# First block sums issued by GpSimd behind output tiles, and attention's token statistics behind a quarter of the second pair's products

## The chip, the core and the metric

The kernel runs on one NeuronCore of a Trainium2 chip. A core has five engines, each with its own in-order stream of instructions: TensorE (PE in the profile, with its weight loads as PEld) multiplies matrices into PSUM, VectorE (DVE) and ScalarE (ACT) do arithmetic on tiles, GpSimd (POOL) does some arithmetic, and SyncE (SP) does nothing but issue DMAs. GpSimd issues DMAs as well; those that add to their destination (accumulate) are issued there. The metric is device microseconds of one launch. A measurement of this kernel spreads over some 0.4%.

## The reference

A decoder trunk of two layers on 512 tokens with 16 learned meta tokens put in front (528 in all), width 1024, everything in float32. Each layer is a mixer and a gated MLP, each behind an RMS norm and added to the residual h:

```python
h = concatenate([meta, x])                      # 528 x 1024
# layer 0: forgetting attention, 16 heads of 64
q, k, v, f, o = split(rms_norm(h) @ w_in)
q, k = rms_norm(q), rms_norm(k)                 # per head
c = cumsum(log_sigmoid(f + b_f))
s = q.k / 8 + c_t - c_s  (causal);  a = softmax(s) v
h = h + (a * sigmoid(o)) @ w_out
# layer 1: HGRN2, 8 heads of 128, chunks of 64
S_t = diag(f_t) S_{t-1} + k_t v_t^T;  o_t = S_t^T q_t;  gated, projected, added to h
# after each mixer: ConvFFN, hidden width 2816
a = causal_conv3(rms_norm(h) @ w_gate)
h = h + (silu(a) * (rms_norm(h) @ w_up)) @ w_down
```

The output is the last 512 tokens of h.

## The kernel before

All of h stays in SBUF as eight tiles of 128 features by 528 tokens. A product of float32 accuracy is made of three fp32r matmuls: weight and input are each split into a high part (a cast on ACT) and a low part (a subtraction on DVE, `sub`, line 126), and hi·hi, hi·lo and lo·hi are summed in PSUM (`proj_unit`, lines 250, 253 and 254). A weight is so loaded (SP), cast (ACT) and subtracted (DVE) before its matmuls run. The raw buffers that the loads write are few, and the next load of a kind waits until the subtraction has read the one before. The tokens' RMS factor is not applied to the input but to the product: `sumsq` adds squares over the eight tiles into `ss`, `token_stats` (lines 350 and 352) sums over the partitions with narrow matmuls, a chain of small DVE operations makes the reciprocal root, and `spread_rs` (line 371) spreads it over partitions into `rsb`.

**Attention** (`fox`) runs over eight pairs of heads. `stage_a(p)` makes q and k of a pair (two weights, two token halves: four PSUM tiles of 24 matmuls each), `stage_v` the values, `stage_f` the forget gates, `stage_l` and `stage_t` the softmax. `weave` deals these generators out against each other: each yields the cost of a step, and the one that has done the smallest share of its stated cost goes next. The tile scheduler then sets the order on each engine by its own rules. Before the first pair, the statistics of the tokens are made: `token_stats`, two more matmuls for the row form (line 430), four DMAs into `et`, and `spread_rs`; all of this stands in the program ahead of pair 0 and waits for the last square of h. The first pair's products have four PSUM tiles of their own, and pair 1's q takes the banks "p" when those come free. At the end, `out_proj(m)` multiplies the gated heads by wo for the eight output tiles in the order m = 4, 0, 1, 2, 3, 5, 6, 7: the tiles 0 to 3 are mostly done already and need a weight of 128 KB each; 4 to 7 take one of 512 KB.

**The MLP** (`ffn`) computes most of its pairs of hidden tiles by Strassen's scheme: seven products of half-size blocks in place of eight (`seven`, lines 1183 to 1185). Four of the seven left operands are sums of two weight blocks. `make_sums` forms them by DMA alone, with no engine's arithmetic: a plain load of one block of 256 KB (line 225, on SP) into a room, then a second block, or an earlier sum, accumulated onto it (line 226, on POOL). A job (one pair's gate or up half) has four sums: 1 and 3 from the weights, 2 as an accumulate of sum 1, 4 as an accumulate of sum 2. There are eleven rooms, used in turn. `make_sums` is a generator that is stepped by `next(self.making)`; a step forms one or two sums. Six steps are taken before the MLP starts: in attention at the start of six of the output tiles, in the HGRN mixer at the start of the output tiles 2 to 7. The further steps are taken inside `seven`, when a job's sums have been cast (line 1160). The first pair of hidden tiles is computed plainly (`plain`, line 1255 is the end of its up half), and Strassen's pairs follow. `new_pair` clears two columns of a tile A on GpSimd (line 1236), in the first MLP only.

## Time and profile before

| | |
|---|---|
| three runs | 1447.70, 1450.93, 1453.36 us |
| the profiled execution | 1452.92 us |
| its span | 1451.1 us, mean granted clock 0.994 |
| PE busy | 1420.7 us (98%) |
| DVE, ACT, POOL busy | 1010.1, 724.3, 164.3 us |
| moved by DMA | 206.9 MB, mean 143 GB/s |

Attention takes the first 392 us of the span, the first MLP up to about 760, HGRN up to about 1096, the second MLP the rest. "Idle before, releaser" in a row is how long the engine stood still ahead of an instruction and what ended that. A DMA's time "to landing" runs from its issue to the last byte. The granted PE clock is given as a share of full speed.

### The profile page before, as it was taken

The numbers are of one execution on the slowest core, as the hardware profiler recorded it, in microseconds if no ns is written. First come the engines' busy times: TensorE is split into PE (matmuls) and PEld (weight loads), VectorE is DVE, ScalarE is ACT, GpSimd is POOL, SyncE is SP. The second block draws the span as 40 slices with busy tenths as digits, with TensorE's granted clock in tenths as the row PEclk, the third lists the DMA queues.
The fourth block names the chain that finished last, engine by engine and source line by source line (L and its number), as shares of the span: only waits on it lengthen the run. The fifth ranks groups of instructions, "written<-read, shape, count | busy, mean of one in ns | idle before, by whom it ended". The sixth has DMA issues, their size and how long they took to land.

```text
span 1451.1 us, 29767 instructions
## 1 busy us (share of the span) xinstructions
PE 1420.7 (98%) x11368; PEld 1339.2 (92%) x11368; DVE 1010.1 (70%) x2282; ACT 724.3 (50%) x1528; POOL 164.3 (11%) x273
## 2 busy tenths in 40 slices
PE   7999999999899999999999999999999999999998
PEld 6898888899899999999999999999999899999997
DVE  6545455775698886767775667677656987777774
ACT  5356554663566554554543224333435665555551
POOL 4000000001012222221000000000100222221100
PEclk9999999999999999999999999999999999999999
DMA  4424344335659898886322202222643899989833
GB/s 161 120 63 134 76 124 123 89 99 150 182 138 232 231 238 203 205 214 165 97 61 87 88 2 88 61 72 74 170 122 84 206 256 220 237 214 222 203 90 101
DMA packets 105463, 206.90 MB, mean 143 GB/s; under 512 B 14168, under 2 KB 18008, under 8 KB 105320
## 3 DMA queue, kind: packets, MB, share of 16 engines
q1 hardware_dynamic: 82280, 163.05, 36.9%
q0 software_dynamic: 23040, 41.95, 17.5%
q8 instruction: 89, 1.46, 0.4%
q14 instruction: 54, 0.44, 0.1%
HBM read 168.53 MB, written 2.10 MB: 118 GB/s over the span
## 4 chain that ended last, share of the span: by engine, by line
PE 91%; DMA 4%; DVE 2%; ACT 2%; SPq 1%; issue 1%; DVEq 0%; ACTq 0%
PE pss L250 7%; PE pss L254 7%; PE pss L253 7%; PE psp L250 7%; PE psp L253 7%; PE psp L254 7%; PE psp L301 6%; PE psp L1183 5%; PE psp L1184 5%; PE psp L1185 5%; PE psd L1183 3%; PE psd L1184 3%; PE psd L1185 3%; PE psc L816 2%; PE pss L974 1%; PE psc L1183 1%
## 5 line engine op out<-in xcount | busy, mean ns | idle before, releaser
L126 DVE TENSOR_TENSOR lo<-raw,hi 128x512 fp32r<-128x512 f32 (+2 forms) x322 | 252.8, 790 | 79.8 <-ACT hi L1160 39.9
L250 PE MATMUL psp<-xhi,hi 128*128 128x264 f32 (+2 forms) x784 | 228.1, 292 | 6.2 <-ACT xhi L326 6.2
L253 PE MATMUL psp<-xlo,hi 128*128 128x264 f32 (+2 forms) x784 | 226.4, 289 | 0.0
L254 PE MATMUL psp<-xhi,lo 128*128 128x264 f32 (+2 forms) x784 | 225.9, 289 | 0.0
L1160 ACT CAST hi<-raw 128x512 fp32r<-128x512 f32 (+1 forms) x232 | 139.2, 604 | 170.4 <-PE pss L253 58.6
L253 PE MATMUL pss<-room,hi 128*128 128x264 f32 (+2 forms) x532 | 169.7, 320 | 0.0
L254 PE MATMUL pss<-room,lo 128*128 128x264 f32 (+2 forms) x532 | 168.8, 320 | 0.0
L250 PE MATMUL pss<-room,hi 128*128 128x264 f32 (+2 forms) x532 | 168.1, 320 | 0.0
L250 PEld LDWEIGHTS psp<-xhi,hi 128*128 128x128 f32 x784 | 149.9, 192 | 9.8 <-ACT xhi L326 6.2
L200 ACT CAST hi<-raw 128x1024 fp32r<-128x1024 f32 (+2 forms) x86 | 83.1, 968 | 145.0 <-PE psp L253 63.9
L253 PEld LDWEIGHTS psp<-xlo,hi 128*128 128x128 f32 x784 | 149.7, 191 | 2.2 <-issue 2.1
L254 PEld LDWEIGHTS psp<-xhi,lo 128*128 128x128 f32 x784 | 149.2, 191 | 2.0 <-issue 1.9
L1183 PE MATMUL psp<-xhi,hi 128*128 128x264 f32 (+1 forms) x480 | 136.4, 284 | 3.4 <-ACT hi L1160 2.7
L1185 PE MATMUL psp<-xhi,lo 128*128 128x264 f32 (+1 forms) x480 | 136.2, 284 | 0.9 <-DVE lo L126 0.9
L1184 PE MATMUL psp<-xlo,hi 128*128 128x264 f32 (+1 forms) x480 | 135.7, 283 | 0.0
L1160 ACT CAST hi<-two 128x512 fp32r<-128x512 f32 x118 | 72.9, 619 | 84.5 <-PE psd L1184 33.0
L254 PEld LDWEIGHTS pss<-room,lo 128*128 128x128 f32 x532 | 100.1, 189 | 6.3
L253 PEld LDWEIGHTS pss<-room,hi 128*128 128x128 f32 x532 | 100.2, 188 | 5.2
L250 PEld LDWEIGHTS pss<-room,hi 128*128 128x128 f32 x532 | 99.5, 188 | 4.2
L1307 DVE TENSOR_TENSOR h<-h,pss 128x264 f32<-128x264 f32 (+2 forms) x145 | 73.6, 508 | 36.3 <-PE pss L254 35.9
L1183 PEld LDWEIGHTS psp<-xhi,hi 128*128 128x128 f32 x480 | 90.7, 189 | 6.5 <-ACT hi L1160 4.0
L1183 PE MATMUL psd<-xfhi,hi 128*128 128x264 f32 (+1 forms) x320 | 90.8, 284 | 1.3 <-ACT hi L1160 0.7
(485 smaller groups left out, 3939.3 us busy)
## 6 DMA issues: line engine op xcount, KB each, us to landing
raw<-gu SPq DMA_DIRECT2D x136, 256.0 KB
two<-gu SPq DMA_DIRECT2D x118, 256.0 KB
raw<-dn SPq DMA_DIRECT2D x80, 256.0 KB
two<-gu POOLq DMA_DIRECT2D x58, 256.0 KB, 6.8
one<-gu SPq DMA_DIRECT2D x42, 256.0 KB
two<-two POOLq DMA_DIRECT2D x40, 256.0 KB, 5.0
pk<-stg SPq DMA_DIRECT2D x30, 264.0 KB
raw<-wqk SPq DMA_DIRECT2D x14, 512.0 KB
```

Source lines behind the costliest of these rows:

```text
L126: self.nc.vector.tensor_tensor(out, x, y, ALU.subtract)
L200: nc.scalar.copy(hi, raw)
L250: ins = mm(ps, hi[:, i, :], xh, start=k == 0, stop=False)
L253: mm(ps, hi[:, i, :], xl, start=False, stop=False)
L254: mm(ps, lo[:, i, :], xh, start=False, stop=k == total - 1)
L301: mm(ps[:tn, :256], y[:, t0 : t0 + tn], w, start=n == 0, stop=n == 23)
L816: ins = mm(o, v[:, j, 2 * (p % 2) + hd, :], w[hd][0], start=j == 0, stop=j == last)
L1160: nc.scalar.copy(hi, raw)
L1183: mm(ps, hi[:, k, :], xh, start=start and k == 0, stop=False, skip_group_check=not start)
L1184: mm(ps, hi[:, k, :], xl, start=False, stop=False, skip_group_check=not start)
L1185: mm(ps, lo[:, k, :], xh, start=False, stop=k == 3, skip_group_check=not start)
L1307: nc.vector.tensor_tensor(hv, hv, ps, ALU.add)
```

## The change

Two things are altered.

*Token statistics.* They become a function `stats` that `stage_a(0)` calls after it has copied its own row of squares, so that they stand behind pair 0's products in the program. Their matmuls get an order (without a semaphore) behind `self.product`, the last matmul that `proj_unit` has written so far. The work of the first two turns of the loop is dealt out by hand: `stage_a(0)` up to a cost of 10.6, then `stage_a(1)` up to 2.6, which is the first of its four PSUM tiles, then the rest of `stage_a(0)`; `stage_a(1)` goes on in the next turn. Pair 1's products take banks "s", as the statistics do, in place of "p".

*Block sums.* While `self.pace` is set, `new` first copies one column of the tile `pace` into the room on GpSimd, and issues the plain load on GpSimd too. The load overwrites the column, so that it has to wait for the copy, and the copy waits for the tile. `pace` is the last column of the output tile of h that has just been done. The steps are taken at the ends of output tiles: five in attention (after tiles 3, 4, 5, 6 and 7, in the order in which they run), five in HGRN (after 0, 2, 4, 6 and 7), and the sixth in `plain` behind its first up half, with `pace` a column of t. Then `pace` is cleared, and the further loads are issued on SP as before. Six steps form nine sums.

```diff
         def new(job, f, x, y):
             s = made[job, f] = next(rooms)
-            nc.sync.dma_start(s, x)
+            if self.pace is None:
+                nc.sync.dma_start(s, x)
+            else:
+
+                nc.gpsimd.tensor_copy(s[:, 0:1], self.pace)
+                nc.gpsimd.dma_start(s, x)
             nc.gpsimd.dma_start(s, y, accum_op=ALU.add)
...
-                mm(ps, lo[:, i, :], xh, start=False, stop=k == total - 1)
+                self.product = mm(ps, lo[:, i, :], xh, start=False, stop=k == total - 1)
...
-            nc.tensor.matmul(ps[:, t, :], self.ss[:, t0 - i0 : t0 - i0 + P], self.onesd, start=True, stop=True)
+            ins = nc.tensor.matmul(ps[:, t, :], self.ss[:, t0 - i0 : t0 - i0 + P], self.onesd, start=True, stop=True)
+            if prev is not None:
+                self.after(ins, prev)
...
-        am, rs = self.token_stats(SEG0, True, start)
         et = sp.tile([64, 33], F32, name="et")
-        ssr = s2.tile([2, T], F32, name="ssr", tag="strow", bufs=1)
-        for t0, tn in full:
-            sr = start()
-            mm(sr[:2, :tn], self.onesd, self.ss[:, t0 : t0 + tn], start=True, stop=True)
-            nc.vector.tensor_copy(ssr[:, t0 : t0 + tn], sr[:2, :tn])
...
+        def stats():
+
+            nonlocal rs
+            _, rs = self.token_stats(SEG0, True, start, self.product)
...
+            self.spread_rs(rs, SEG0, start)
...
-                    ps = banks[i] if banks else bank()
+                    ps = banks[i] if banks else start() if p == 1 else bank()
...
             yield 0.9
+            if p == 0:
+                stats()
...
-            if p + 3 < NPAIR:
+            if p == -3:
+
+                first, second = stage_a(0), stage_a(1)
+                fill += [take(first, 10.6), take(second, 2.6), first]
+                cost += 15.5
+            elif p == -2:
+                fill.append(second)
+                cost += 10.2
+            elif p + 3 < NPAIR:
...
-            for step, _ in enumerate(out_proj(m, 6 if m < NEARLY else 0, KT, res)):
-                if i > 1 and step == 0:
-                    next(self.making)
+            for _ in out_proj(m, 6 if m < NEARLY else 0, KT, res):
+                pass
             self.sumsq(m, first=NEARLY)
+            self.pace = self.h[:, m, T - 1 :]
+            if m >= NEARLY - 1:
+                next(self.making)
...
         for m in range(KT):
-            if m > 1:
-                next(self.making)
...
             self.sumsq(m, A1)
+            self.pace = self.h[:, m, T - 1 :]
+            if m in (0, 2, 4, 6, 7):
+                next(self.making)
...
                 input_forms(2 * m + 1)
+                self.pace = t[:, 0, n - 1 : n]
+                if m == 0:
+                    next(self.making)
+            self.pace = None
             split(t, out)
```

How the instructions stand now, at three places. First TensorE at the start, where pair 0's products end (psd); before, the statistics (pss from ss) follow at once:

```order
L250 MATMUL psd<-xhi,hi 128x264
L253 MATMUL psd<-xlo,hi 128x264
L254 MATMUL psd<-xhi,lo 128x264
L350 MATMUL pss<-onesd,ss 128x2 x5
L352 MATMUL pss<-onesd,ss 16x2
L430 MATMUL pss<-ss,onesd 2x264 x2
L544 MATMUL psd<-sqq,hsel 32x264
L250 MATMUL psp<-xhi,hi 128x264
```

and in the changed kernel, behind 24 rows of products into pss of which these are the last three, and ahead of the values (line 306):

```order
L255 MATMUL pss<-xhi,hi 128x264
L258 MATMUL pss<-xlo,hi 128x264
L259 MATMUL pss<-xhi,lo 128x264
L355 MATMUL pss<-onesd,ss 128x2 x5
L359 MATMUL pss<-onesd,ss 16x2
L443 MATMUL pss<-ss,onesd 2x264 x2
L559 MATMUL psd<-sqq,hsel 32x264
L306 MATMUL psp<-hi,xhi 128x256
```

The statistics moved back by 24 products. Lines 350, 352, 430 and 544 of before are 355, 359, 443 and 559 of the change. From the first MLP on, TensorE's order is the same in both.

Second SP's queue at the end of attention (wo is the output weight, gu the gate and up weights; `one` and `two` hold the rooms), before:

```order
L199 DMA raw<-wo 128x256
L225 DMA one<-gu 128x512
L199 DMA raw<-wo 128x256 x2
L199 DMA raw<-wo 128x1024
L225 DMA two<-gu 128x512 x2
L199 DMA raw<-wo 128x256
L225 DMA two<-gu 128x512 x6
L199 DMA raw<-wo 128x256 x3
L724 DMA res<-h 128x528
L199 DMA raw<-wo 128x1024 x3
```

and now:

```order
L226 DMA one<-gu 128x512 x2
L199 DMA raw<-wo 128x256 x2
L199 DMA raw<-wo 128x1024
L199 DMA raw<-wo 128x256 x4
L749 DMA res<-h 128x528
L199 DMA raw<-wo 128x1024 x3
```

Eleven loads of sums stood among the wo weights; two are left, ahead of them, and nine have gone to GpSimd. In HGRN the same nine have left the places between that mixer's output weights.

Third GpSimd's queue from there on, before, where each row is the accumulate of a sum, with the clears of A:

```order
L226 DMA one<-gu 128x512
L226 DMA two<-gu 128x512 x4
L226 DMA two<-two 128x512
L226 DMA two<-gu 128x512
L226 DMA two<-two 128x512 x2
L226 DMA one<-two 128x512 x2
L1236 MEMSET A 128x2x2 x2
```

and now the last step of the nine, the one that waits for t:

```order
L229 COPY two<-t 128x1
L229 COPY one<-t 128x1
L230 DMA two<-gu 128x512
L230 DMA one<-gu 128x512
L231 DMA two<-two 128x512
L231 DMA two<-gu 128x512
L231 DMA one<-gu 128x512
L231 DMA two<-two 128x512
L231 DMA one<-two 128x512
L231 DMA two<-gu 128x512
L231 DMA two<-one 128x512
L1264 MEMSET A 128x2x2
```

Line 229 is the paced copy, 230 the plain load, 231 the accumulate. All later accumulates and clears stand behind these copies in the same queue.

More of the change, by code (lines that the diff above doesn't have):

```diff
@@ L343, in rsqrt, with token_stats @@
         return y
-    def token_stats(self, segs, last=False, bank=None):
+    def token_stats(self, segs, last=False, bank=None, prev=None):
         nc = self.nc
@@ L349, in token_stats @@
         for t, (t0, _, i0, _) in enumerate(segs):
-            nc.tensor.matmul(ps[:, t, :], self.ss[:, t0 - i0 : t0 - i0 + P], self.onesd, start=True, stop=True)
+            ins = nc.tensor.matmul(ps[:, t, :], self.ss[:, t0 - i0 : t0 - i0 + P], self.onesd, start=True, stop=True)
+            if prev is not None:
+                self.after(ins, prev)
         if last:
-            nc.tensor.matmul(ps[:16, 5, :], self.ss[:, 512:528], self.onesd, start=True, stop=True)
+            ins = nc.tensor.matmul(ps[:16, 5, :], self.ss[:, 512:528], self.onesd, start=True, stop=True)
+            self.after(ins, prev)
         am = self.cp.tile([P, 6], F32, name="am", tag="am", bufs=2)
@@ L424, in fox @@
         start = partial(self.bank, "s")
-        am, rs = self.token_stats(SEG0, True, start)
         et = sp.tile([64, 33], F32, name="et")
-        ssr = s2.tile([2, T], F32, name="ssr", tag="strow", bufs=1)
-        for t0, tn in full:
-            sr = start()
-            mm(sr[:2, :tn], self.onesd, self.ss[:, t0 : t0 + tn], start=True, stop=True)
-            nc.vector.tensor_copy(ssr[:, t0 : t0 + tn], sr[:2, :tn])
-        for g in range(4):
-            t0, tn = full[g % 2]
-            nc.sync.dma_start(et[16 * g : 16 * g + 16, :], ssr[:, t0 : t0 + tn].rearrange("r (j c) -> r j c", c=33))
-        nc.vector.tensor_scalar(et, et, EPS, EPS, ALU.add, ALU.mult)
-        self.spread_rs(rs, SEG0, start)
+        rs = None
+        def stats():
+            nonlocal rs
+            _, rs = self.token_stats(SEG0, True, start, self.product)
+            ssr = s2.tile([2, T], F32, name="ssr", tag="strow", bufs=1)
+            for t0, tn in full:
+                sr = start()
+                ins = mm(sr[:2, :tn], self.onesd, self.ss[:, t0 : t0 + tn], start=True, stop=True)
+                self.after(ins, self.product)
+                nc.vector.tensor_copy(ssr[:, t0 : t0 + tn], sr[:2, :tn])
+            for g in range(4):
+                t0, tn = full[g % 2]
+                nc.sync.dma_start(et[16 * g : 16 * g + 16, :], ssr[:, t0 : t0 + tn].rearrange("r (j c) -> r j c", c=33))
+            nc.vector.tensor_scalar(et, et, EPS, EPS, ALU.add, ALU.mult)
+            self.spread_rs(rs, SEG0, start)
         rcol = [0, 1, 2, 3, 5]
```

## The prediction

> **What bounds the kernel now.** I read the page's busy times and chain first, then the PE timeline for every idle stretch, then the windows and the DMA rows round each of them.
>
> ```profile
> PE 1420.7 (98%) x11368; PEld 1339.2 (92%) x11368; DVE 1010.1 (70%) x2282; ACT 724.3 (50%) x1528; POOL 164.3 (11%) x273
> PE 91%; DMA 4%; DVE 2%; ACT 2%; SPq 1%; issue 1%; DVEq 0%; ACTq 0%
> ```
>
> TensorE is the bound. The span is 1451.1 us and PE is busy for 1420.7 of it, so all idle time together is 30 us, the first 6.2 of it before anything has landed. A change that adds no matmul, as this one, can only take or give PE idle time, and time at the reduced clock. The matmuls named here stand where that idle time is (its length and its releaser in brackets):
>
> ```profile
> 20.64 0.28 PE L254 MATMUL psd<-xhi,lo 128*128 128x264 f32 x1
> 23.61 1.28 PE L350 MATMUL pss<-onesd,ss 128*128 128x2 f32 x10 [2.69 <-DVE ss L318]
> 68.11 0.38 PE L483 MATMUL psc<-tot,cst 128*128 128x2 f32 x2 [1.40 <-DVE tot L481]
> 187.10 0.44 PE L779 MATMUL pss<-identr,lr 128*128 128x128 f32 x1 [1.96 <-DVE rqq L342]
> 270.24 0.36 PE L573 MATMUL psd<-rows,selr 128*128 128x264 f32 x1 [1.57 <-DMA rows<-yr]
> 363.76 0.39 PE L250 MATMUL pss<-pk,hi 128*128 128x264 f32 x1 [1.38 <-ACT hi L200]
> 368.68 0.39 PE L250 MATMUL psp<-pk,hi 128*128 128x264 f32 x1 [1.41 <-ACT hi L200]
> 372.57 0.39 PE L250 MATMUL pss<-pk,hi 128*128 128x264 f32 x1 [2.15 <-ACT hi L200]
> ```
>
> Some of these idle stretches cost twice. In the windows below the columns are busy time and count of PE, PEld, DVE, ACT and POOL, then the granted PE clock, the DMA share and the GB/s.
>
> ```profile
> 22.50:25.80 3.30, 2.19 (x17) 1.64 (x18) 3.20 (x10) 2.96 (x8) 0.00 (x0) 1.00 0.48 161
> 25.80:29.20 3.40, 3.40 (x16) 1.91 (x14) 3.03 (x20) 0.15 (x1) 0.00 (x0) 0.50 0.01 1
> 29.20:32.60 3.40, 3.40 (x32) 3.15 (x27) 1.00 (x4) 0.38 (x1) 0.00 (x0) 1.00 0.01 2
> 66.70:70.10 3.40, 2.00 (x17) 1.99 (x17) 3.09 (x15) 1.42 (x3) 0.00 (x0) 1.00 0.67 225
> 370.60:374.00 3.40, 0.82 (x5) 0.61 (x5) 3.40 (x7) 2.53 (x4) 0.48 (x1) 0.99 1.09 274
> 374.00:377.40 3.40, 3.40 (x16) 3.40 (x17) 3.40 (x5) 1.91 (x3) 0.00 (x0) 0.50 0.89 245
> ```
>
> After the gaps at 23.61 and at 372.57 the clock is 0.50 for one stretch of 3.4 us. That stretch holds 16 matmuls where the next one at full clock holds 32, so it costs about 1.7 us of PE time. After 66.7 to 70.1, which was busy for 2.00 us, the clock stayed at 1.00; before the half stretch at 25.8 it was 2.19 us, nearly all of it the narrow statistics matmuls. So what decides is how little work the stretch before held, the limit lies near 2 us of 3.4, and small matmuls seem to count for less. The Trainium skill ("TensorE: Matmul & The Clock Gate", What's actually happening) has a free-running window of about 3.4 us after which an idle array is halved; the length agrees with the 3.4 us here, but these windows were only partly idle, and the measurement decides. Were only a wholly idle window punished, the clock terms below would be nothing, and the sum 3.4 us poorer.
>
> **The start: token statistics behind 24 products.** The statistics matmuls (L350) waited for the last sum of squares while PE had run dry. Now 24 products of the second pair stand between. One product is 0.12 us after the other at full clock (32 matmuls in 3.4 us come to 0.11), so they take about 2.9 us. What they need:
>
> ```profile
> 17.41 1.23 DVE L126 TENSOR_TENSOR lo<-raw,hi 128x1024 fp32r<-128x1024 f32 x1 [0.22 <-ACT hi L200]
> 22.05 1.51 DVE L318 TENSOR_TENSOR ss<-ss,sq 128x528 f32<-128x528 f32 x2
> ```
>
> The second pair's q weights are split by 17.41 + 1.23 = 18.64, before PE ends its first products at 20.92 (20.64 + 0.28), and the new bank comes from the pool that the statistics also use, empty so far. They run 20.92 to 23.8, and the sum is ready at 23.56: the 2.69 us gap is filled with work that PE has to do anyway. Gain 2.7 us. The half-clock stretch at 25.8 goes if 24 full products lift the stretch before it over the limit; the 12 small statistics matmuls are still in it. I take it as gone, 1.7 us, since a stretch busy for 2.00 us kept its clock; the bounds are 2.7 and 4.4. What stands later now: everything that needs the token scale (the spread matmuls, the forget gate) is some 3 us later in PE's order but is reached at the same distance behind its inputs, and the first values fill PE meanwhile. Cost nothing; if the values' weights were not split (they are the third split of 1.2 us on DVE), up to 1 us.
>
> **The rest of attention** changes its order only because work is dealt out by shares. The gaps at 68.11, 187.10 and 270.24 (4.9 us together) and half-clock stretches after the last two hang on small DVE chains and row DMAs whose partners move. No row says which way. From below, all of it could go (about 9 us with three half-clock stretches of 1.7); from above, as much again could come. I take nothing, and 3 us either way for the range.
>
> **Attention's end: where the sums' loads were.** Before, eleven block sums were issued during the out-projection, 22 transfers of 256 KB, on SP ahead of the out-projection's own weights. The chain of waits and the DMA rows (KB, then median us to landing; first the window 338 to 346, then 349 to 375):
>
> ```profile
> 354.31 8.89 DMA raw<-wo
> 364.19 3.93 DMA raw<-wo
> one<-gu POOLq DMA_DIRECT2D x1, 256.0 KB, 4.3
> two<-gu POOLq DMA_DIRECT2D x5, 256.0 KB, 7.7
> 350.00:365.00 15.00, 13.62 (x113) 12.91 (x112) 6.93 (x15) 3.64 (x5) 6.07 (x7) 1.00 1.01 251
> ```
>
> The DMA engines are full (1.01), an accumulate of 256 KB takes 7.7 us where it took 4.3 with room, and a wo weight of 128 KB takes 8.89 us. With nine of the loads moved behind output tiles (two stay on SP), at the ratio 4.3/7.7 that weight needs about 5.0 us and lands at 359.3; with cast and split (0.4 us each) it is ready before PE stops at 362.4 (363.76 less 1.38). Each next weight waits for the buffer of the one before, so the gaps at 368.68 and 372.57 move forward with it by the same 3.9 us and more than close. Gain 1.38 + 1.41 + 2.15 = 4.9 us, and 1.7 us for the half-clock stretch after 370.6 to 374, which was busy for 0.82 us: 6.6 us. The lower bound is 2, if the paced sums (the first pair of loads goes out when the first output tile is done, while seven wo weights are still to come) cost the weights half of it.
>
> **The price: the sums come later.** The loads of the first two jobs (seven of the nine) go out as the output tiles end, from about 359 to 392, some 5 to 35 us later than before. The first cast of a sum stands at 405.49, so with a landing and an accumulate of 7.7 us each (392 + 17 = 409 for the last, which is not the first one cast) they cost nothing. The last step of the table is the tight one: two loads behind the first up-projection's t (L1255), and in series on POOL: copy, load, landing, accumulate, landing; then the second sum of that job is an accumulate of the first, and another one of the second. Their casts and the first matmul that uses the second and the last of them:
>
> ```profile
> 411.63 0.87 POOL L226 DMA_DIRECT2D two<-gu  x1 [18.18 <-DMA two<-gu]
> 405.49 0.62 ACT L1160 CAST hi<-two 128x512 fp32r<-128x512 f32 x1 [0.83 <-PE pss L253]
> 423.53 0.77 DVE L1255 TENSOR_TENSOR t<-pss,t 128x264 f32<-128x264 f32 x2
> 441.19 0.61 ACT L1160 CAST hi<-one 128x512 fp32r<-128x512 f32 x1
> 444.65 0.60 ACT L1160 CAST hi<-two 128x512 fp32r<-128x512 f32 x1
> 447.82 0.28 PE L1183 MATMUL psc<-xfhi,hi 128*128 128x264 f32 x1
> 451.11 0.29 PE L1183 MATMUL psp<-xhi,hi 128*128 128x264 f32 x1
> 425.00:450.00 25.00, 23.06 (x184) 22.43 (x184) 21.89 (x40) 16.19 (x33) 5.24 (x7) 1.00 0.90 210
> 437.81 0.10 POOL L1236 MEMSET A<- 128x4 f32 x1 [1.04 <-DVE t L1218]
> 466.36 0.83 ACT L1214 ACTIVATE t<-A,vec 128x528 f32<-128x528 f32 x1 [0.53 <-DVE A L1272]
> 1130.90 0.68 DVE L1255 TENSOR_TENSOR t<-pss,t 128x512 f32<-128x512 f32 x1
> 1149.12 0.61 ACT L1160 CAST hi<-one 128x512 fp32r<-128x512 f32 x1
> 1149.63 0.62 ACT L1160 CAST hi<-two 128x512 fp32r<-128x512 f32 x1
> 1152.27 0.28 PE L1183 MATMUL psc<-xfhi,hi 128*128 128x258 f32 x1
> 1153.93 0.28 PE L1183 MATMUL psp<-xhi,hi 128*128 128x258 f32 x1
> ```
>
> First FFN: t is written at 424.3, the copy of one column I take as 0.1, each issue on POOL is 0.87. With landings of 4.3 us: first sum 424.3 + 0.1 + 0.87 + 4.3 + 0.87 + 4.3 = 434.7, the second 5.2 later at 439.9, the last at 445.1: on time but for 0.4. With 7.7 throughout, and both loads issued first: 442.4, 451.0 and 459.5; with 1.3 us for cast and split, the last is late for PE by 9.7 us. Halfway (about 5.5, the stretch is 0.90 busy) the last is ready at about 452, 1 us late. I take 1.
>
> Second FFN: t ends at 1131.6, 7.3 us closer to the last cast. Low: 1142.0, 1147.2, 1152.4; ready 1153.7 against 1153.93, no loss. High: 1149.7, 1158.3, 1166.8, late by 14. Halfway: 1145.3, 1151.7, 1158.0, some 5 us late. Since a sum that is late holds only its own product and PE's order has down-products of other pairs round it, and the low landings were measured with the stretch before half empty, I take 3. At the end of the second mixer, where nine loads leave SP as well, PE has no gap that they could close: gain nothing there.
>
> Queued behind the waiting copies on POOL are the accumulates, counted above, and the clears of the next A. The clear that stood at 437.81 comes behind the third job's last accumulate now, at 460 by the high bound, and its reader starts at 466.36: nothing.
>
> **Sum.** 1452.92 (the profiled execution, 2.0 above the median of the runs) − 4.4 − 6.6 + 1 + 3 = 1445.9. Against the median of 1450.93 the same −7.0 gives **1443.9 us**.
>
> **Rivals.**
> 1. *Late sums set the end* (the other side). Mechanism: the chain copy, load, accumulate, accumulate on POOL for the third job of each FFN. It decides once a landing there takes more than about 6.1 us, where the two prices together (3 and 8) eat the whole gain. For it: the 0.90 DMA share at 425 to 450, into which four more sums (2 MB, 9 us at 210 GB/s) are now pushed; against it: the 4.3 us landing. At 7.7 us: +9.7 + 14 + one half-clock stretch each (3.4) − 11 = +16, so up to 1467 on the median; about 1461 at 7. The Trainium skill ("SBUF — State Buffer", SBUF: two separate sides) warns that a DMA issued by GpSimd can starve while DVE holds the port they share; it would push the same way. The trace speaks against: an issue took 0.87 us at 411.63 amid busy DVE. Chance 0.13.
> 2. *The clock and the shares give it back.* The half-clock stretch at the start stays (the small matmuls are still there), or a new one comes in attention, and the wo weights keep half of their delay: −2.7 − 3.3 + 4, about 1448.9. For it: the limit near 2 us that two windows straddle. Chance 0.22.
> 3. *The start is filled but the wo weights still come late*, because SP issues them no earlier than their buffers come free: −4.4 − 2 + 2, 1446.5. For it: the casts wait for DMA and the loads for the cast, in turn; against it: 8.89 us is a landing, not a wait for a buffer. Chance 0.13.
> 4. *The forecast*, with its gains in full and the price between 0 and 5: 1440 to 1445. Chance 0.52; of it 0.46 lies under the 0.5% line.
>
> 0.5% is about 7.3 us, what a measurement of this kernel can tell from no change. Faster than 1443.7: 0.46 from the forecast and 0.03 from attention's order falling well, 0.49. Slower than 1458.2: from the first rival 0.08, and 0.03 from attention falling badly: 0.11. The rest, 0.40. The range reaches from 1437 (full gains, no price, 2 us from attention) to 1453, which leaves out the worse half of the first rival.
>
> **What would show it.** Right: no idle time ahead of the statistics matmuls and clock 1.00 at 25.8; no wait of PE for a wo cast between 350 and 375; first sums on POOL spread over 350 to 395. Wrong: casts of sums in 435 to 455 and 1140 to 1160 that waited for a DMA, with PE idle behind them; DMA share over 1 in these stretches; new half-clock stretches in attention.

## The result

| | before | changed |
|---|---|---|
| runs | 1447.70, 1449.52, 1450.93, 1453.36 us | 1464.35, 1464.71, 1469.44, 1469.77 us |
| median | 1450.22 us | 1467.08 us |
| profiled execution | 1452.92 us | 1469.77 us |

The ratio is 1.0115, with a 95% interval from 1.0083 to 1.0147: the change makes the kernel 1.15% slower. The forecast was 1443.9 us, within 1437 to 1453. The time lies above that range, on the other side of before, at the upper end of what the first rival was given. Both profiled executions are 2.7 us above the medians of their kernels, so the difference of the two stands for that of the medians.

The page of the changed kernel (the line of busy times):

```profile
PE 1429.2 (97%) x11368; PEld 1347.5 (92%) x11368; DVE 1010.4 (69%) x2282; ACT 723.6 (49%) x1528; POOL 180.8 (12%) x309
```

The span grew by 16.9 us (1468.0 less 1451.1). PE has the same 11368 matmuls and is busy for 8.5 us more (1429.2 less 1420.7), and idle for 8.4 more (38.8 against 30.4). So half of the loss is waiting, and the other half is the same matmuls taking longer, at a mean granted clock of 0.986 where it was 0.994.

**Where it lies** is seen best by matmuls: the start of a matmul in the changed kernel, less the start of the one that has as many still to come in the kernel before. The columns are the places in the kernel before; the rows are profiled executions (of some experiments too, by their numbers below; negative is earlier than before).

| at (us of before) | 50 | 150 | 340 | 400 | 520 | 1130 | 1300 |
|---|---|---|---|---|---|---|---|
| the change | -6.15 | +9.65 | +3.23 | +0.81 | +6.49 | +6.49 | +16.62 |
| statistics alone (1) | -5.95 | +6.69 | -0.63 | -1.55 | -1.04 | -1.02 | -0.08 |
| sums alone (2) | -1.03 | -0.88 | -4.21 | -10.27 | -5.57 | -5.57 | +3.77 |
| sums alone, sixth step early (5) | -1.07 | -0.50 | -3.17 | -10.61 | -10.39 | -10.39 | -10.12 |
| the change, two mends (12) | -6.13 | +0.32 | -4.68 | -11.20 | -10.04 | -9.05 | -8.64 |

Read along the first row: the start gives some 6 us, the middle of attention takes 9.4 back, attention's end gives 2.4, the first MLP takes 5.7, HGRN nothing, and the second MLP takes 10.1.

PE's idle stretches in the changed kernel, with length and releaser (the first row stands for the statistics, which have no idle time ahead of them now):

```profile
22.97 1.17 PE L355 MATMUL pss<-onesd,ss 128*128 128x2 f32 x10
72.10 0.28 PE L771 MATMUL pss<-pk 66*128 66x16 f32 x1 [2.24 <-DMA pk<-cneg]
83.16 0.59 PE L590 MATMUL psd<-rows,selr 128*128 128x264 f32 x1 [1.58 <-DVE rawk L591]
373.61 0.59 PE L255 MATMUL pss<-pk,hi 128*128 128x264 f32 x1 [2.98 <-ACT hi L200]
444.83 0.39 PE L1211 MATMUL psd<-xfhi,hi 128*128 128x264 f32 x1 [2.24 <-ACT psd L1224]
486.42 0.39 PE L1211 MATMUL psd<-xfhi,hi 128*128 128x264 f32 x1 [2.40 <-DVE part L1322]
1154.83 0.58 PE L1211 MATMUL psd<-xfhi,hi 128*128 128x258 f32 x1 [2.99 <-ACT psd L1224]
1166.71 0.58 PE L1211 MATMUL psc<-xfhi,hi 128*128 128x258 f32 x1 [4.57 <-ACT psc L1218]
```

And its windows, with the columns of the prediction's:

```profile
25.80:29.20 3.40, 3.40 (x30) 2.90 (x30) 1.06 (x8) 0.38 (x1) 0.00 (x0) 1.00 0.01 1
68.90:72.30 3.40, 1.16 (x10) 0.95 (x9) 1.88 (x8) 1.67 (x4) 0.00 (x0) 1.00 0.65 239
72.30:75.70 3.40, 3.40 (x17) 2.94 (x17) 2.13 (x6) 1.88 (x9) 0.00 (x0) 0.50 0.05 9
82.60:86.00 3.40, 2.13 (x11) 1.00 (x12) 2.52 (x9) 2.56 (x8) 0.22 (x2) 0.50 0.01 2
123.50:126.90 3.40, 3.40 (x15) 2.75 (x15) 1.60 (x10) 0.72 (x4) 0.00 (x0) 0.50 0.40 115
350.00:365.00 15.00, 15.00 (x128) 14.36 (x125) 8.98 (x22) 6.29 (x14) 0.46 (x3) 1.00 0.21 69
372.70:376.10 3.40, 2.49 (x11) 2.49 (x12) 3.40 (x5) 2.03 (x3) 1.20 (x2) 0.50 0.98 173
425.00:450.00 25.00, 20.82 (x163) 19.87 (x162) 19.03 (x36) 13.11 (x26) 10.12 (x15) 1.00 1.01 230
1150.00:1170.00 20.00, 12.44 (x75) 11.72 (x74) 11.29 (x19) 7.99 (x19) 4.35 (x5) 0.78 0.88 198
```

Half clock after the start is gone, as is the DMA load at 350 to 365 (0.21 where it was 1.01). New half-clock stretches stand in attention from 72.3, 82.6 and 123.5. At 425 to 450 the DMA share rose from 0.90 to 1.01 and PE's busy time fell from 23.06 to 20.82 us. The second MLP's stretch is the worst: PE is busy for 12.44 of 20 us, at a clock of 0.78. In the kernel before it was busy throughout, with DMA engines that were fuller (1.02 against 0.88):

```profile
1150.00:1170.00 20.00, 20.00 (x156) 19.40 (x155) 19.19 (x35) 13.25 (x29) 4.35 (x5) 1.00 1.02 255
```

**What is late in the MLPs.** ACT's casts ahead of these gaps, with what they waited for, and two copies that follow them on ACT (lines 1218 and 1224 carry one product's PSUM bank into the next one's):

```profile
442.83 0.62 ACT L1188 CAST hi<-raw 128x512 fp32r<-128x512 f32 x1 [4.71 <-DMA raw<-gu]
445.50 0.62 ACT L1188 CAST hi<-one 128x512 fp32r<-128x512 f32 x1 [0.41 <-DMA one<-two]
450.01 0.62 ACT L1188 CAST hi<-two 128x512 fp32r<-128x512 f32 x1 [0.92 <-DMA two<-one]
484.65 0.92 ACT L1188 CAST hi<-raw 128x512 fp32r<-128x512 f32 x2 [6.60 <-DMA raw<-dn]
1153.88 0.62 ACT L1188 CAST hi<-raw 128x512 fp32r<-128x512 f32 x1 [3.34 <-DMA raw<-gu]
1154.41 0.37 ACT L1224 COPY psd<-psc 128x258 f32<-128x258 f32 x1
...
1165.05 0.62 ACT L1188 CAST hi<-two 128x512 fp32r<-128x512 f32 x1 [5.11 <-DMA two<-one]
...
1166.30 0.36 ACT L1218 COPY psc<-psp 128x258 f32<-128x258 f32 x1
```

The DMA rows in the chain of waits (start, us to landing):

```profile
68.43 3.63 DMA pk<-cneg
367.26 5.17 DMA raw<-wo
435.79 7.02 DMA raw<-gu
476.88 7.69 DMA raw<-dn
1151.06 8.18 DMA one<-two
1159.53 5.45 DMA two<-one
```

In the first MLP the sums held ACT for less than 1 us each (0.41 and 0.92); what came late were plain weights, the gate-and-up weight at 435.79 and the down weight at 476.88, in a stretch whose DMA engines are full. In the second MLP a weight was late first (1153.88), and then the last sum of the third job (1165.05), for which ACT stood 5.11 us. The two accumulates at 1151.06 and 1159.53, one behind the other, took 8.18 and 5.45 us.

PE's own rows name neither: at 1154.83 it waited for the copy of line 1224 and at 1166.71 for that of line 1218, each 0.4 us long. These copies belong to products that are not the late block's, and stood behind its cast in ACT's queue. At 486.42 the same goes through DVE, which had its subtraction behind the late cast, and `part` behind that.

### The profile page after: what moved, and what is told of

The parts are those of the page before. It is cut to its first block, busy times and chain, and to the rows that moved or that the text cites. A ratio compares the mean times of both kernels' runs of the same rounds, so it can differ in the third digit from the quotient of the medians.

```text
span 1468.0 us, 29780 instructions
## 1 busy us (share of the span) xinstructions
PE 1429.2 (97%) x11368; PEld 1347.5 (92%) x11368; DVE 1010.4 (69%) x2282; ACT 723.6 (49%) x1528; POOL 180.8 (12%) x309
## 4 chain that ended last, share of the span: by engine, by line
PE 91%; DMA 4%; DVE 2%; ACT 1%; issue 1%; SPq 1%; POOL 0%; DVEq 0%; ACTq 0%; POOLq 0%
PE pss L255 8%; PE pss L258 8%; PE pss L259 8%; PE psp L255 7%; PE psp L258 7%; PE psp L259 7%; PE psp L306 6%; PE psp L1211 5%; PE psp L1213 5%; PE psp L1212 5%; PE psd L1211 2%; PE psd L1212 2%; PE psd L1213 2%; PE psc L843 2%; PE pss L1001 1%; PE psc L1211 1%
## 5 line engine op out<-in xcount | busy, mean ns | idle before, releaser
L255 PE MATMUL psp<-xhi,hi 128*128 128x264 f32 (+2 forms) x752 | 219.5, 293 | 7.2 <-ACT xhi L331 6.1
L259 PE MATMUL psp<-xhi,lo 128*128 128x264 f32 (+2 forms) x752 | 218.7, 291 | 0.0
L258 PE MATMUL psp<-xlo,hi 128*128 128x264 f32 (+2 forms) x752 | 218.4, 291 | 0.0
L255 PEld LDWEIGHTS psp<-xhi,hi 128*128 128x128 f32 x752 | 144.7, 193 | 10.7 <-ACT xhi L331 6.1
L258 PEld LDWEIGHTS psp<-xlo,hi 128*128 128x128 f32 x752 | 144.8, 193 | 1.5 <-issue 1.4
L259 PEld LDWEIGHTS psp<-xhi,lo 128*128 128x128 f32 x752 | 144.4, 192 | 2.0 <-issue 1.9
L1211 PEld LDWEIGHTS psp<-xhi,hi 128*128 128x128 f32 x480 | 91.5, 191 | 6.6 <-ACT hi L1188 4.0
```

Of the source, the lines that this page charges most:

```text
L255: ins = mm(ps, hi[:, i, :], xh, start=k == 0, stop=False)
L258: mm(ps, hi[:, i, :], xl, start=False, stop=False)
L259: self.product = mm(ps, lo[:, i, :], xh, start=False, stop=k == total - 1)
L1211: mm(ps, hi[:, k, :], xh, start=start and k == 0, stop=False, skip_group_check=not start)
```

## The experiments

Times are medians; ratios are to the kernel before, measured alongside, with 95% intervals. Medians of different experiments have their own measurements of before (1450.4 to 1452.0 us), so that differences of 1 or 2 us between them say little.

**1. The statistics alone**: all of the sums' part undone, in the main

```diff
-            if self.pace is None:
-                nc.sync.dma_start(s, x)
-            else:
-
-                nc.gpsimd.tensor_copy(s[:, 0:1], self.pace)
-                nc.gpsimd.dma_start(s, x)
+            nc.sync.dma_start(s, x)
```

> Only the token statistics and the second pair's first quarter are moved; the sums are as before. Theory (the loss sits in the two MLPs, where the sums' DMA traffic now is): attention ends within 3 us of before (4.4 us won at the start, lost again to other gaps and half-clock stretches), both MLPs as before, 1448 to 1455 us in all. Rival (the loss comes from attention's new order and its half-clock stretches): most of the 17 us is here, 1460 us or more.

Measured: 1459.1 us, ratio 1.0043 [1.0028, 1.0058], about 6 us slower, between the two. Neither was right: the statistics cost nearly as much in the middle of attention as they give at the start. The profiled execution was the fastest of seven (1452.51), so its row in the table above shows too little of the loss.

**2. The sums alone**: the statistics and the dealt-out work as before, the paced sums kept.

```diff
+        am, rs = self.token_stats(SEG0, True, start)
...
-            if p == 0:
-                stats()
...
-            if p == -3:
-
-                first, second = stage_a(0), stage_a(1)
-                fill += [take(first, 10.6), take(second, 2.6), first]
...
-            elif p + 3 < NPAIR:
+            if p + 3 < NPAIR:
```

> Only the sums are paced and issued by GpSimd; the statistics are as before. Theory: about 0 to 1 us won at attention's end, 5 to 6 us lost in the first MLP and 10 in the second, 1463 to 1467 us. Rival (attention's order carries the loss): 1452 us or less.

Measured: 1456.87 us, ratio 1.0042 [1.0029, 1.0055]; neither again. The table tells why: here attention's end gives 6.1 us (from -4.21 to -10.27), and the MLPs then take 4.7 and 9.3. PE and ACT of this kernel:

```profile
435.97 0.39 PE L1191 MATMUL psp<-xhi,hi 128*128 128x264 f32 x1 [2.67 <-ACT A L1281]
1143.59 0.39 PE L1191 MATMUL psd<-xfhi,hi 128*128 128x258 f32 x1 [3.83 <-ACT psd L1204]
1154.52 0.58 PE L1191 MATMUL psc<-xfhi,hi 128*128 128x258 f32 x1 [3.37 <-ACT psc L1198]
```

```profile
435.00 0.62 ACT L1168 CAST hi<-one 128x512 fp32r<-128x512 f32 x1 [3.16 <-DMA one<-two]
1142.65 0.62 ACT L1168 CAST hi<-raw 128x512 fp32r<-128x512 f32 x1 [4.16 <-DMA raw<-gu]
1152.87 0.62 ACT L1168 CAST hi<-two 128x512 fp32r<-128x512 f32 x1 [4.93 <-DMA two<-one]
```

The MLPs lose 14 us here and 15.8 with the statistics: that price belongs to the sums. Each part alone costs about 6 us and both together 17; the table has most of the rest at attention's end, where the sums give 6.1 alone and 2.4 in the change. Ahead of two of its three gaps ACT stood for a late sum, ahead of one for a late weight.

**3. The change with the sixth step at the mixers' ends**: the step that waited for t is taken behind the last output tile and waits for that; the loads of all later steps are on SP, as in the change.

```diff
+        next(self.making)
+        self.pace = None
...
-                self.pace = t[:, 0, n - 1 : n]
-                if m == 0:
-                    next(self.making)
-            self.pace = None
```

> The change, but the sixth step of the sums (the third job's sums 1 and 3) is taken at the end of the mixer, behind the last output tile, and not behind the first product of the plain pair. Theory (the third job's transfers fall into a stretch in which the DMA engines are full): PE's gaps of 2.2 and 2.4 us in the first MLP and of 3.0 and 4.6 us in the second are gone or under 1 us, 1451 to 1456 us. Rival (issue by GpSimd, or the pacing of the first five steps, is what costs): the gaps stay, 1462 us or more.

Measured: 1453.77 us, ratio 1.0020 [1.0009, 1.0030], the time that the first theory had. The longest wait of PE in the two MLPs' stretches is 1.33 us now (at 1144.27; the theory asked for none over 1), and 13 us of the 17 are gone. The rest is in attention.

**4. The kernel before with nine loads issued by GpSimd**, no copy and no wait added: which engine issues, by itself.

```diff
-            nc.sync.dma_start(s, x)
+            (nc.gpsimd if self.early else nc.sync).dma_start(s, x)
```

> The kernel before, but the nine loads of the first six steps are issued by GpSimd at their old places in the program, without the copy that holds them. Theory (which engine issues a load does not matter, only when): 1448 to 1454 us, wo weights late by 8 to 9 us as before. Rival (loads on GpSimd are slower, since its queue is in order with the accumulates or its descriptors are written late): 1456 us or more, with later sums.

Measured: 1450.67 us, ratio 1.0001 [0.9992, 1.0011]. For these nine loads, which stand at the mixers' ends, the issuing engine is worth nothing. The DMA share at 350 to 365 stayed at 1.08 there, so what empties this stretch in the change is the wait, not the engine.

**5. The sums alone with the sixth step early** (2 and 3 together).

> Statistics as before; sums paced and issued by GpSimd, the sixth step at the end of the mixer. Theory (pacing wins at attention's end, the late sixth step loses in the MLPs, and the statistics' order loses in attention): attention ends 6 to 10 us earlier than before, no PE gap over 1 us in either MLP, 1442 to 1447 us. Rival (paced first five steps cost in the MLPs as well, or the sixth step now delays the last wo weight): 1450 us or more.

Measured: 1444.22 us, ratio 0.9951 [0.9936, 0.9967]: faster, as the first theory said. PE is at most 0.6 us short in these windows, at attention's end and in the MLPs:

```profile
350.00:365.00 15.00, 14.49 (x117) 14.08 (x116) 10.95 (x24) 7.12 (x13) 1.73 (x4) 1.00 0.43 147
425.00:450.00 25.00, 24.41 (x201) 24.20 (x199) 22.41 (x41) 17.05 (x36) 5.44 (x8) 1.00 0.96 236
1150.00:1170.00 20.00, 20.00 (x154) 19.34 (x153) 17.74 (x34) 12.84 (x27) 4.20 (x5) 1.00 0.99 246
```

Against experiment 2, one step of the table moved ahead of the MLP is worth 12.7 us. The MLPs run some 10 us earlier here. At 415 to 440, the place of 425 to 450 before, PE is busy for 23.06 us, just as before; the longest wait in the second MLP is 1.35 us, at 1136.30, where the theory asked for none over 1. The DMA share of 0.96 and 0.99 comes with hardly any PE time lost, so a full stretch alone does not make PE wait. Two experiments ask what part of the loss is traffic.

**6 and 7. Traffic added to experiment 5**: six stores of 256 KB in each MLP, into the output, which the results overwrite later; nothing of the computation is left out. First with `xfhi` as their source:

```diff
+                if m == 0:
+                    for i in range(6):
+                        x = xfhi[:, 0:2, 1, :].bitcast(F32)
+                        nc.gpsimd.dma_start(a["out"][i].rearrange("p (f t) -> p f t", f=2), x[:, :, 0:256])
```

> The kernel e5 with all sums on time, plus six stores of 256 KB each from a finished tile to parts of the output that are written again later, issued by GpSimd behind the first product of the plain pair: the late transfers' traffic without late sums. Theory (in the first MLP it is the traffic that delays the plain weights): PE waits of 2 us or more for a raw weight return near 435 and near 1150, 3 to 8 us above e5. Rival (only the chain copy, load, accumulate, accumulate makes PE wait): within 2 us of e5.

Measured: 1445.26 us, ratio 0.9961 [0.9949, 0.9974]. It decides nothing: the source was ready early, and the stores left from 401.3 and 1110 on, ahead of the tight stretches. The second try takes them from t, where they have to wait for the plain pair:

```diff
+                if m == 0:
+                    for i in range(6):
+                        nc.gpsimd.dma_start(a["out"][i], t[:, 0, :512])
```

> The kernel e5 with all sums on time, plus six stores of 256 KB of t itself to parts of the output that are written again later, issued by GpSimd: they cannot start before the first product of the plain pair is multiplied, so that they lie where the change's late transfers lie (e6's stores went out some 15 us earlier). Theory (traffic alone delays the plain weights): PE waits of 2 us or more near 425 or near 1145, 3 to 8 us above e5's 1444. Rival (only sums that come late make PE wait): within 2 us of it.

Measured: 1446.12 us, ratio 0.9955 [0.9938, 0.9972], 1.9 us above experiment 5, which is inside the 2 us that the rival was given, and by the ratios (0.9955 and 0.9951) not clear of noise. The stores went out in place and took 6.6 us in the median, and PE waits where it did in the change, for less:

```profile
472.30 0.39 PE L1195 MATMUL psd<-xfhi,hi 128*128 128x264 f32 x1 [1.18 <-DVE part L1305]
1140.22 0.39 PE L1195 MATMUL psd<-xfhi,hi 128*128 128x258 f32 x1 [2.50 <-ACT psd L1208]
```

The second of these waits is 1.35 us without the stores. By the starts of the matmuls, as in the table, the two MLPs take 1.8 and 1.4 us here (from 400 to 520 and from 1130 to 1300) and 0.2 and 0.3 in experiment 5. So 1.5 MB of transfers pushed into each stretch cost some 2.7 us in these two executions, a small part of the 12.7; the medians do not confirm it. They are not the same transfers as the late sums' (stores, where the sums add into SBUF), so what accumulates would cost as traffic alone was not measured.

**8 and 9. The order of the tiles at attention's end.** The gap at 373.61 comes because PE's order starts tile 6 (four matmuls of the high part) ahead of the other 44 of tile 5, and tile 6's weight was issued only at 367.26, when DVE had read the last 128 KB weight out of its buffer (366.82 + 0.42). A wait in order (no semaphore) of each late tile behind the one before:

```diff
+            prev = self.score if hold else self.product if m > NEARLY else None
...
-                yield from self.proj_unit(ps[:, :tn], [wt], ox[k0:k1], t0, tn, self.score if hold else None)
+                yield from self.proj_unit(ps[:, :tn], [wt], ox[k0:k1], t0, tn, prev)
```

On experiment 3:

> The kernel e3 (the change with the sixth step early), with TensorE held to the order of the output tiles 5, 6, 7: no matmul of a tile ahead of the last of the tile before. Theory (PE stands 2.8 us at tile 6's first four matmuls, which the order puts ahead of 44 matmuls of tile 5 that are ready): the gap and most of the 6.8 us at half clock behind it go, 4 to 6 us less than e3, 1448 to 1450 us. Rival (the weight's landing binds whatever the order, so the gap only moves to tile 6's start): within 2 us of e3.

On experiment 5:

> The same order of the output tiles on the kernel e5. Theory: the wait for tile 7's weight (0.9 us in the run with the sums alone) goes, 1 to 2 us less than e5, about 1442 to 1445 us. Rival: no difference that can be told.

Measured: 1452.43 us, ratio 1.0007 [0.9994, 1.0021], and 1444.04 us, ratio 0.9953 [0.9934, 0.9971]: 1.3 us less, with intervals that overlap, and no difference, where I had asked for 4 to 6 on experiment 3. There the gap only moved, to the low part of tile 5: PE, and DVE ahead of it, which did a normalisation (from 367.68) and an output tile (from 368.36) first:

```profile
369.97 0.39 PE L259 MATMUL pss<-pk,lo 128*128 128x264 f32 x1 [2.09 <-DVE lo L126]
```

```profile
368.70 1.22 DVE L126 TENSOR_TENSOR lo<-raw,hi 128x1024 fp32r<-128x1024 f32 x1
```

**10. The statistics alone, with a larger stated cost of the forget gates.** A generator with a larger stated cost is behind by share and goes sooner. It came from three rows of DVE in the changed kernel:

```profile
64.45 0.20 DVE L501 CAST cneg<-w 128x66 fp32r<-128x66 f32 x1
67.80 0.19 DVE L569 TENSOR_TENSOR am<-am,et 64x33 f32<-64x33 f32 x1 [3.15 <-DMA am<-strow]
67.91 0.21 DVE L126 TENSOR_TENSOR cneg<-w,cneg 128x66 fp32r<-128x66 f32 x1
```

The low part of `cneg` (the sums of the forget gates) was ready to be made at 64.65, but stood behind `am`, which waited 3.15 us for its own row DMA. `cneg` left at 68.43, landed 3.63 us later, at 72.06, and PE waited for it until 72.10.

```diff
-                (stage_f() if p == -2 else None, 3.5),
+                (stage_f() if p == -2 else None, 5.0),
```

> The statistics moved alone (as e1), but the forget gates' generator gets a larger share (5.0 for 3.5), so that it is dealt out earlier; then DVE has the low part of cneg ahead of the row am, which waits for a DMA, as it was before the change and is not in e1. Theory (the statistics' order loses its 4.4 us again because the forget gates' last operation on DVE stands behind a wait for a DMA, which leaves PE idle at 72 and brings half-clock stretches after it): no PE gap over 1 us between 65 and 85, no half-clock stretch there, 1447 to 1452 us. Rival (the half-clock stretches come from the new order elsewhere): as e1, 1456 us or more.

Measured: 1452.41 us, ratio 1.0004 [0.9994, 1.0014], 6.7 us less than experiment 1 (5.7 by the ratios), just above what was expected. The wait for `cneg` is gone; a gap of 3.26 us at 82.80 is there, where the theory asked for none over 1. The time is that of before and no better: by the starts of the matmuls this kernel is 5.4 us ahead at 340 and 1.9 at 400. Attention's end, where the sums are still in the way of wo, takes the rest, with gaps of 3.02 and 2.44 us.

**11. All three mends on the change** (3, 8 and 10).

> The change with three mends: the sixth step early (e3), the output tiles in order (e7), the forget gates earlier (e9). Theory (the gains of both parts then stand side by side): 1440 to 1445 us, faster than e5. Rival (the statistics' order also spoils the end of attention, where e3 lost 2.8 us of idle time and a half-clock stretch that e5 does not have): 1447 us or more.

Measured: 1442.09 us, ratio 0.9927 [0.9912, 0.9942].

**12. Without the order of the tiles** (3 and 10).

> The change with the sixth step early and the statistics' share forgotten at 5.0, without the order of the tiles at attention's end. Theory that the tiles' order is worth little by itself (1454 to 1452 beside the sixth step alone) and that the statistics' share is the mend that counts: 1441 to 1445, within 2 us of the version with all three mends (1442.1), and a gap of 2 to 3 us at tile 6 near 373 may come back. Rival, that the order counts once the half-clock stretches of the statistics are gone: 1446 to 1450.

Measured: 1442.0 us, ratio 0.9932 [0.9916, 0.9949]. The order of the tiles is worth nothing that can be told; two mends are enough, and both versions beat the kernel before, by 0.7%. Most of that is the sums': experiment 5 has 0.9951 with the old statistics, and its interval overlaps with this one's, so that the moved statistics gain anything is not shown. DVE, PE and ACT of this one:

```profile
61.67 0.23 DVE L126 TENSOR_TENSOR cneg<-w,cneg 128x66 fp32r<-128x66 f32 x1
67.43 0.19 DVE L569 TENSOR_TENSOR am<-am,et 64x33 f32<-64x33 f32 x1 [4.28 <-DMA am<-strow]
```

```profile
82.14 0.59 PE L255 MATMUL psp<-xhi,hi 128*128 128x264 f32 x1 [3.17 <-ACT rawq L551]
370.07 0.39 PE L255 MATMUL psp<-pk,hi 128*128 128x264 f32 x1 [0.70 <-ACT hi L200]
```

```profile
80.66 1.04 ACT L200 CAST hi<-raw 128x1024 fp32r<-128x1024 f32 x1 [3.64 <-DMA raw<-wv]
81.61 0.85 ACT L551 ACTIVATE rawq<-psp,qg 128x264 f32<-128x264 f32 x2
```

`am` still waits, for 4.28 us, and `cneg` is ahead of it; PE's wait for it is down to 0.23 us. The gap at 82.14 is another case of the same kind: ACT stood 3.64 us for a values weight (wv), and the copy that frees PE's bank stood behind that cast. Experiment 10 has the same rows, with 3.73 us at 81.33. The change itself does not have this gap; its idle time at 83.16 is 1.58 us and hangs on DVE. From experiment 3 this one edit takes 1.0020 to 0.9932, about 12 us by the medians, and the gap at attention's end fell to 0.70 with it. The edit moves all of the forget gates, so it shows that the place of the forget gates in the order is what counts. How much of the 12 us is the single wait for `cneg`, and why the last gap closes too, was not taken apart. The edit was not tried on the kernel before either, whose own gap at 68.11 has the same origin (below), so part of its worth may have nothing to do with the moved statistics.

## Why the prediction was wrong

The forecast was −4.4 at the start, 0 in the rest of attention, −6.6 at attention's end, +1 and +3 for the price: −7. By the table the change did −6.2, +9.4, −2.4, +5.7 and +10.1: +16.6.

1. **The start: right.** No idle time ahead of the statistics at 22.97, the clock 1.00 at 25.8 to 29.2. The stretch from 22.5 to 25.8 was busy throughout, for 3.30 us. By 50 us the change is 6.15 ahead, but the six other profiled kernels with the old statistics lie between 1.9 ahead and 1.4 behind there, so about 5 us is the statistics' own. Three of those six (experiments 4, 7 and 9) have no half-clock stretch after their statistics: the 1.7 us for it was a matter of the execution.

2. **The rest of attention: "I take nothing" failed.** The step that fell is that what depends on the statistics "is reached at the same distance behind its inputs". On DVE the chain of the norm (`am`) came to stand between two halves of the forget gates' chain and, in order, held the second for a DMA that had nothing to do with it. The 16 us between 50 and 150 lie in PE's 2.24 us of idle time for it and in the half-clock stretches from 72.3, 82.6 and 123.5; the first of these follows that wait directly, and that the other two hang on it is not shown. Against this stands that the gaps of the kernel before at 187 and 270 don't come back, which leaves +9.4. The one at 270 is no merit of the change: in experiments 4 and 5, with attention's start as before, it is 0.53 and 0.57 us and no half clock follows. The kernel before already has the hold on DVE, ahead of the gap at 68.11 that the prediction put down to "small DVE chains":

```profile
66.31 0.19 DVE L552 TENSOR_TENSOR am<-am,et 64x33 f32<-64x33 f32 x1 [4.10 <-DMA am<-strow]
67.89 0.17 DVE L481 COPY tot<-w 128x2 f32<-128x2 f32 x1
```

   The forget gates' totals (`tot`) stood there behind `am`, and PE waited 1.40 us for them, so a row that warns of this was on hand. (The expectation of experiment 10 has the order of before the other way round: `cneg` came after `am` there too, at 70.78.) The bound of 3 us either way was too small by its own working, which had 9 us on both sides. Experiment 10 with 1 shows that some 6 us hang on the order of the forget gates, and in 12 the middle costs 1.5 us with it (from −6.13 to −4.68).

3. **Attention's end: right in size, but only without the statistics' order.** The DMA load went from 1.01 to 0.21, the four 128 KB weights were in time, and the sums alone gave 6.1 to 7.4 us here (experiments 2 and 5) where 6.6 was forecast. In the change itself it came to 2.4. "The gaps at 368.68 and 372.57 move forward with it and more than close" failed for the second: tile 6's weight could be issued only at 367.26, when DVE had freed a buffer, and landed 5.17 us later, so PE waited 2.98 us at 373.61 and ran at half clock after it. That is the third rival's mechanism (SP issues no earlier than a buffer comes free), at one tile.

4. **The price: the step that decides the sign.** 4 was forecast, 15.8 measured. It has three faults.
   - *The discount.* In the second MLP the halfway estimate had the last sum landed at 1158, some 5 us late. Moved on by the 6.49 us that the changed kernel was behind at 1130, that is 1164.5; by its rows the sum landed at 1164.98 (1159.53 + 5.45). So the end of the chain was right to about 0.5 us, but by luck, since its terms erred both ways: the copies on POOL held the first load for 1.8 us, to 1141.52, where I had put down 0.1, and the landings put at 5.5 us were 4.42, 4.28, 8.18 and 5.45. But I took 3 for it since "a late sum … holds only its own product". It held ACT: its cast at 1165.05 stood for 5.11 us in an in-order queue, the copy of line 1218 behind it, and PE for 4.57 us for that copy. The down-products of other pairs that were to fill PE stood behind in PE's order.
   - *The weights.* The step counted what the traffic does to the sums, not to the weights that share the stretch. In the first MLP the sums were all but in time, and 5.7 us went to a gate-and-up weight of 7.02 us and a down weight of 7.69. Of the four gaps in the MLPs one has a late sum ahead of it and three a late weight.
   - *The clock.* The half stretches behind these gaps (1154.3 and from 1164.6 on) were counted in the rival, not in the forecast.

   One misreading changed nothing. "7.3 us closer to the last cast" does not come out of its rows: from t to the cast of the last sum are 20.4 us in the first MLP and 18.0 in the second, 2.3 closer. The sums do not use it.

   POOL's copies, in the second MLP of the changed kernel (spans on POOL are rough):

```profile
1139.72 1.50 POOL L229 COPY two<-t 128x1 f32<-128x1 f32 x1
1139.84 2.65 POOL L229 COPY one<-t 128x1 f32<-128x1 f32 x1
```

5. **The rivals.** The first had the place and the sign, at a chance of 0.13, but its 1467 is met by luck: it priced the MLPs at 27 us, where they took 15.8, and had no loss in attention, where the middle took 9.4 and the gain at the end fell from 6.6 to 2.4. It was written as late sums only; the runs show late sums and late weights together. New half-clock stretches in attention are from the second rival. Experiment 3 shows the first rival's place, the step that waits for t. Moving that one step ahead of the MLP gives back 13 us of 17 (and 12.7 without the statistics). Its warning sign stood in the prediction, the share of 0.90 into which 2 MB were to go; against it I set one landing of 4.3 us from a half-empty stretch, where the same rows had 7.7 for a full one. A port held on GpSimd's side as the reason for late landings finds no support: with GpSimd issuing the same nine loads the time was 1.0001 of before. That run has none of them in the MLPs; in the changed kernel the two loads of the sixth step landed after 5.45 and 5.54 us in the first MLP and after 4.42 and 3.79 in the second.

Left open are how the loss in the MLPs parts between the late sums and the traffic of the accumulates, and by which steps the order of the forget gates reaches the stretch at 123.5 and attention's end.

## What to carry to other kernels

Moving transfers away from a stretch that they choke was worth here what the gaps there said (6.1 and 7.4 us in experiments 2 and 5, 6.6 forecast), but only if the place they go to has room for them and for the loads already there: work out the landings of both, at the pace of a full stretch, and put no more than the trace shows to be free ahead of the first use. A wait on an in-order queue costs what stands behind it, here small PSUM copies on ACT behind a cast, and half of the forget gates on DVE behind a norm, so when a chain is moved or made late, list on each engine whose instructions it stands in front of. Where two changes are made as one, time each alone: here each lost for a reason of its own; moving one step mended the sums into a gain, and one number brought the statistics back to no loss.

## What the runs showed of the chip

- In these traces the half clock follows stretches of 3.4 us that are only partly idle, and the limit isn't one number of busy time. In the changed kernel 1.16 us busy at 68.9 to 72.3 was followed by 0.50; the stretch from 82.6, busy for 2.13 us and itself at 0.50, was followed by 0.50 again; in the kernel before, a stretch busy for 2.00 us was followed by full clock. The Trainium skill ("TensorE: Matmul & The Clock Gate", What's actually happening) speaks of a window in which the array is idle; here a window with 10 matmuls in it was punished.
- Where the stretches begin differs between executions, and can decide. Experiment 1 has the change's wait at 72 us (2.26 us for 2.24), but its stretches (laid off from its half-clock stretch, 81.48 to 84.89) meet at 71.24, in the midst of the wait. They were busy for 2.23 and 2.33 us, and the clock stayed at 1.00, where the change had 1.16 and then 0.50. So one gap can cost a half-clock stretch or none; whether this makes the executions of experiment 1 (1452.51 to 1460.09 us) and of the change differ was not tested.
- An accumulate of 256 KB took from 4.2 us (two<-one at 445.71) to 8.18 us (at 1151.06) within one execution, so that a chain of two or three of them is uncertain by its own length.
- A copy of one column on GpSimd took 0.4 to 0.5 us at 425.81 and 426.02, and 1.50 and 2.65 at 1139, by the profile's rough spans.
